# One of two row scalings of a retention output moved from the retention stage into the attention stage of a hybrid encoder block

## The chip, the cores and the metric

The kernel runs on one core of a Trainium2 chip. A core has five engines, each with an instruction queue of its own that it works off in order: PE (TensorE, matrix products), DVE (VectorE), ACT (ScalarE), POOL (GpSimd) and SP (SyncE, which here issues all DMAs). They wait for one another by semaphores. The metric is the device time of one execution in microseconds; the median of three runs is given.

## The reference

One encoder block over 1024 frames plus 16 meta tokens, model width 1024, float32. The input is normalised and projected to a retention group (4 heads, key width 64, value width 128) and a forgetting-attention group (8 heads of width 64); their outputs stand side by side in a mixer output of width 1024 that is projected back. A gated feed-forward network with a short convolution and a last normalisation follow.

```python
def hybrid_mixer(h, w_in, forget_b, ret_norm_g, w_out, valid):
    proj = jnp.einsum('bld,de->ble', h, w_in)
    rq, rk, rv, rg, fq, fk, fv, ff = jnp.split(proj, SPLIT_POINTS, axis=-1)
    o_r = retention(rq..., rk..., rv..., valid)              # (B, L, 4, 128)
    o_r = o_r * lax.rsqrt(jnp.mean(o_r * o_r, axis=-1, keepdims=True) + EPS)
    o_r = o_r.reshape(B, L, RET_V) * ret_norm_g * jax.nn.silu(rg)
    log_f = jax.nn.log_sigmoid(ff + forget_b)
    o_f = forgetting_attention(fq..., fk..., fv..., log_f, valid)
    mixed = jnp.concatenate([o_r, o_f], axis=-1)
    return jnp.einsum('ble,ed->bld', mixed, w_out)
```

The change concerns the factor `rsqrt(mean(o_r * o_r))` of head 1. The kernel keeps `o_r` transposed, 128 value features on the partitions and time along the free axis, so this factor is one row of 1026 numbers (the 1024 frames and the two positions ahead of them that the convolution reaches back to) that multiplies all 128 partitions.

## The kernel before, in words

All matrix products are made in float32 precision from two parts: a rounded high part and the difference to it, the low part, in three products (high by high, high by low, low by high). ACT makes the high parts, DVE or POOL the low parts.

The program has these stages, in order of time.

1. **Projections and retention of heads 0 and 1** (`retention(0, ...)`), to about 95 us.
2. **Gates of heads 0 and 1** (`gate(0, ...)`, `gate(1, ...)`) with the end of the first retention (`fin()`): it squares each head's output, sums the squares over the partitions on POOL (`head_sum`, L241, PARTITION_ALL_REDUCE, in halves of 513), and turns the sums into the row `ro` of reciprocal roots by a trip through DRAM (`head_rstd`, L247 to L250). `gate` writes the gated head, not yet scaled, to the DRAM tensor `mix`.
3. **Row scalings** (`scale_rows`, L525 to L530) of heads 0 and 1: load `mix` (tile `sraw`), load the row `ro` repeated on all partitions (tile `src`), multiply on POOL (L529), store to the DRAM tensor `mixg`. Both tiles come from `stage`, a pool of two buffers. Head 1's tiles therefore take the buffers of head 0's.
4. **Retention of heads 2 and 3** (`retention(1, ...)`), from about 105 to 195 us. It runs over four blocks of time (the first one with an extra tile of 16 meta tokens). Per block it projects with `rv_hi`/`rv_lo` into `psj` (L183 to L185), turns and rotates queries and keys, multiplies keys with queries into `psq` (L355, L356), weighs the scores by the decay on DVE (`sf`, two buffers, L361), splits them into `sh` (ACT) and `sl` (POOL, L118), and multiplies these with the values into `psv` (L376 and L377 with `sh`, L378 with `sl`).
5. **Forgetting attention** (from about 195 us), with the projections of its heads spread between its steps (`dense`, L667 and after). It begins with the column sums of heads 2 and 3 on POOL, whose result tiles come from the two buffers of the tag `o`; later the heads' outputs `o` use the same two buffers. `prep_k`, `prep_q` and `max_step` prepare head 0; `load_m` reads all rows of `mixg` near the stage's end.
6. **Rest of the output projection, feed-forward network and last normalisation**, from about 560 us to the end.

Stages 1 to 4 are put in order by a scheduler, which simulates the engines with costs of its own and takes what is ready; so a change of one engine's work changes how the others' queues are interleaved. In stages 5 and 6 the queues of PE, DVE, ACT and POOL keep the order of the program text, while SP's DMAs are still placed by the scheduler.

Of the kernel before, what the change touches and what calls it, by code (L numbers as in the profile page):

```python
# [10 lines left out]
F32 = mybir.dt.float32  # L11
# [6 lines left out]
P = 128  # L18
# [4 lines left out]
NQ = NT - Q0  # L23
# [58 lines left out]
def tile_hymba_block(ctx, tc, xt, xn, wrv0, wrv1, wft, wout, wup, wdn, small, cst, rope, dtab, out):  # L82
# [3 lines left out]
    def f(t):  # L86
        return t.bitcast(F32)

    def mk(es, name, bufs=1, **kw):
        return es.enter_context(tc.tile_pool(name=name, bufs=bufs, reuse_waits="tile", **kw))  # L90
# [10 lines left out]
    def bank(pl):  # L101
        n = names[id(pl)]
        return pl.tile([P, 512], F32, tag=n, name=n)
# [47 lines left out]
    def stage(nm, dt=F32):  # L151
        return sp_.tile([P, NT], dt, tag="st", name=nm)
# [87 lines left out]
    def head_sum(h, rs_, sq, c_):  # L240
        pool.partition_all_reduce(rs_, sq, P, bass_isa.ReduceOp.add)  # L241
        sp.dma_start(ro_d[h][:, c_], rs_[0:1, :])
# [271 lines left out]
    def gate(h, gt, o, late=False):  # L514
        for ps, (a, n) in proj_t(load_ft(f"rg{h}", (dve, pool)[GL[h]], lx[-1] if h == 0 else None), CX_Q, Q0):
            dve.tensor_tensor(gt[:, a:a + n], ps, rb[:, Q0 + a:Q0 + a + n], op=ALU.mult)
        act.activation(gt, gt, AF.Silu)
        if late:
            sp.dma_start(o, ro_d[h].to_broadcast([P, NQ]))
            dve.tensor_tensor(gt, gt, o, op=ALU.mult)  # L520
            sp.dma_start(o, mix_d[h])
        dve.scalar_tensor_tensor(gt, gt, sm[:, S_RG + h:S_RG + h + 1], o, op0=ALU.mult, op1=ALU.mult)
        sp.dma_start(mixg_d[h] if late else mix_d[h], gt)

    def scale_rows(k):  # L525
        raw, rc = stage("sraw")[:, :NQ], stage("src")[:, :NQ]
        sp.dma_start(raw, mix_d[k])
        sp.dma_start(rc, ro_d[k].to_broadcast([P, NQ]))
        pool.tensor_tensor(raw, raw, rc, op=ALU.mult)  # L529
        sp.dma_start(mixg_d[k], raw)  # L530
# [5 lines left out]
    def w_dma(u):  # L536
        if u < len(units_w):
            nm = units_w[u]
            src = wout[int(nm[2])] if nm[:2] == "wo" else wft[:, FX[nm]:FX[nm] + KT * P]
            raws[u] = []  # L540
            for hf in range(2):
                n = (NA - 4) * P if nm[:2] == "wo" and int(nm[2]) < EARLY and hf else 512
                raw = wf.tile([P, 512], F32, tag="raw", name="f_raw", bufs=RB)
                sp.dma_start(raw[:, :n], src[:, hf * 512:hf * 512 + n])
                raws[u].append((raw, n // P))
# [2 lines left out]
    fin()  # L548
    wt1 = [load_rv(1, wr, bb, k) for k in range(KT)]
    gate(1, stage("gate")[:, :NQ], ots[1])  # L550
    for k in range(2):
        scale_rows(k)
    w_dma(0)
    retention(1, wt1, None)[0]()
    ra.close()
# [11 lines left out]
    fp = mk(fa, "fp", 1, side="right")  # L567
# [7 lines left out]
    for s in range(2):  # L575
        o = 64 - 64 * s
# [17 lines left out]
    def w_split(u):  # L594
        if u < len(units_w):
            wts[u] = []
            for raw, n in raws.pop(u):
                h = wg.tile([P, 4, P], F32R, tag="fh", name="f_hi")
                l = wg.tile([P, 4, P], F32R, tag="fl", name="f_lo")
                split(h[:, :n], l[:, :n], raw.rearrange("p (a b) -> p a b", b=P)[:, :n], dve)  # L600
                wts[u].append((h, l))
# [96 lines left out]
    def prep_k(h):  # L698
        p, s = divmod(h, 2)
        h_, o_ = HS[s], HS[1 - s]  # L700
        prep_c(h)
        act.copy(kB[s][h_], kst[p][h_])
        dve.tensor_tensor(k1[s][o_], kst[p][h_], f(kB[s])[h_], op=ALU.subtract)
        dup[0] = sp.dma_start(f(k1[s])[h_], f(kB[s])[h_])
# [8 lines left out]
    def prep_q(h):  # L713
        p, s = divmod(h, 2)
        h_, o_ = HS[s], HS[1 - s]
        c = slice(Q0, NT)
        act.copy(q1[s][h_, c], qst[p][h_, c])
        sp.dma_start(f(qm[s])[h_, c], f(q1[s])[h_, c])
        dve.tensor_tensor(qB[s][h_, c], qst[p][h_, c], f(q1[s])[h_, c], op=ALU.subtract)
        dup[0] = sp.dma_start(f(q1[s])[o_, c], f(q1[s])[h_, c])  # L720

    def max_step(h, j):
        s = h % 2
        t0, R = KTILES[j]
        q_ = Q0 if j == 0 else 0
        w = min(NT, P * j + P)
        for ci, a in enumerate(range(0, w, 512)):
            n = min(512, w - a)
            last = a + n == w
            ps = bank(pS)  # L730
            pe.matmul(ps[:R - q_, :n], lhsT=qm[s][:, t0 + q_:t0 + R], rhs=kB[s][:, a:a + n], start=True, stop=not last)  # L731
            if last:
                pe.matmul(ps[:R - q_, n - R:n], lhsT=msk[:, q_:R], rhs=idr[:, :R], start=False, stop=True)
            dve.tensor_reduce(mxs[s][:R - q_, j, ci:ci + 1], ps[:R - q_, :n], axis=mybir.AxisListType.X, op=ALU.max)  # L734

    def max_end(h):
        s = h % 2
        mf = fp.tile([P, 9], F32, tag="mf", name="mf", bufs=2)
        dve.tensor_reduce(mf, mxs[s], axis=mybir.AxisListType.X, op=ALU.max)
        m2 = fp.tile([P, 2, 9], F32R, tag="m2", name="m2", bufs=2)  # L740
        dve.tensor_scalar(m2[:, 0, :], mf, -1.0, None, op0=ALU.mult)
        dve.scalar_tensor_tensor(m2[:, 1, :], mf, -1.0, f(m2)[:, 0, :], op0=ALU.mult, op1=ALU.subtract)
        return m2

    def max_rows(h, m2):
        s = h % 2
        T = bank(pT)
        pe.transpose(T[:18, :P], f(m2).rearrange("p a b -> p (a b)"), idf)
        mr = fp.tile([18, P], F32, tag="mr", name="mr", bufs=1)
        act.copy(mr, T[:18, :P])  # L750
        sp.dma_start(md[s].rearrange("i (j p) -> (i j) p", p=P), mr)
        o = 64 - 64 * s + 3
        sp.dma_start(f(qB[s])[o:o + 2, Q0:P], md[s][:, 0:P - Q0])
        dup[0] = sp.dma_start(f(qB[s])[o:o + 2, P:NT], md[s][:, P:NT])
# [176 lines left out]
    def run(upto):  # L931
        while done[0] < upto:
            c = next(dn, 0)
            if c == 0:
                done[0] = 1 << 60
            done[0] += c
# [12 lines left out]
    with tc.manual_schedule(engines=ENG):  # L949
        for s_ in range(2):  # L950
            rs_ = fp.tile([P, NQ], F32, tag="o", name="rss", bufs=2)
            head_sum(2 + s_, rs_, sqs[s_], slice(0, NQ))
        w_split(0)
        run(U + 161)
        prep_q(0)
        run(2 * U + 1)
        prep_k(0)
        for j in range(9):
            run(2 * U + V * (j + 5) // 15)
            max_step(0, j)  # L960
        run(2 * U + V * 14 // 15)
        m2 = max_end(0)
        prep_k(1)
        prep_q(1)
        run(2 * U + V + 1 + U // 8)
        max_rows(0, m2)
        run(GOAL[0])
        for h in range(2, 4):
            head_rstd(h)
        for t in range(len(units) + LAG):  # L970
            h, at = divmod(t, NU)
            if h < 7:
                want = GOAL[h] + (GOAL[h + 1] - GOAL[h]) * (at + 1) // NU
            else:
                want = GOAL[7] + (END - GOAL[7]) * (t - 7 * NU + 1) // (NU + LAG)
            run((done[0] + want) // 2)
            if h == 6 and at == 4:
                fqs.close()
                wA[0] = mk(fqs, "wA", side="right")
            if h == 6 and at == 4:  # L980
                m7 += [mt[7][:, 0, :], mt[7][:, 1, :]]
            if h == 6 and at == 12:
                load_m(6, mt[6])
            if h == 7 and at == 4:
                split_m(6)
            if t < len(units):
                part_s(t)
            if 0 <= t - 1 < len(units):
                part_d(t - 1)
            if 0 < h and at == 6:  # L990
                norm1(h - 1)
            if 0 < h and at == 10:
                norm2(h - 1)
            if t < len(units):
                if h < 7:
                    if at == 0 and h > 0:
                        prep_q(h + 1)
                    if at == 1 and h > 0:
                        prep_k(h + 1)
                    for j in range(9):  # L1000
                        if SPLIT[j] == at:
                            max_step(h + 1, j)
                    if at == SPLIT[8]:
                        m2 = max_end(h + 1)
                    if at == SPLIT[8] + 1:
                        max_rows(h + 1, m2)
            run(want)
            if t - LAG >= 0:
                part_v(t - LAG)
        run(1 << 50)  # L1010
# [826 lines left out]
```

## Time and profile before

| | |
|---|---|
| timed runs | 1337.38, 1339.93, 1330.31 us; median 1337.38 |
| profiled execution | 1337.85 us, of it the span from first to last instruction 1334.9 us |
| PE busy | 1272.2 us (95% of the span) |
| DVE, ACT, POOL busy | 925.9, 588.0, 378.0 us |
| mean granted PE clock | 0.972 |
| the two row scalings on POOL | 2.39 us at 125.77 and 2.34 us at 137.59 |

In a row of a timeline stand the start and the length in us, the engine, the line of the kernel, the operation, output `<-` inputs, the shapes, and in brackets how long the engine had been idle before and what released it. "issue" as a releaser means that the profile shows none. A row of waits has who waited, for whom, the total in us, how often, and the longest. The granted clock is the share of full speed at which PE was allowed to run.

### The profile page before, as it was taken

The page shows a single profiled execution, that of the slowest core. Times are in us where ns is not written, and L with a number is a line of the kernel's source. Part 1 is how long each engine was busy: PE and PEld are TensorE (multiplying, and loading weights), DVE is VectorE, ACT ScalarE, POOL GpSimd, SP SyncE. Part 2 cuts the span into 40 slices and gives each one's busy share as a digit, 9 for nine tenths or more (in the row PEclk, how much of TensorE's full clock was granted, in tenths as well). Part 3 has the DMA queues.
Part 4 walks back from the last instruction along what each step waited for, and adds up shares of the span by engine and source line. Part 5 has one row for each costly group of instructions (what it writes and reads, how often), then busy time and mean ns, then how long its engine had stood idle before and what let it go on. Part 6 is the DMA issues. An engine that isn't in the chain of part 4 may idle for free.

```text
span 1334.9 us, 24161 instructions
## 1 busy us (share of the span) xinstructions
PE 1272.2 (95%) x9243; PEld 1202.9 (90%) x9243; DVE 925.9 (69%) x1573; ACT 588.0 (44%) x1162; POOL 378.0 (28%) x308
## 2 busy tenths in 40 slices
PE   9999799999999989988799999999999998999995
PEld 8999799999999989977699999999999997888884
DVE  5774456555665666647878878879889885955566
ACT  7763251445355554532443433433433435444553
POOL 0163235000000000033336545546546540500123
PEclk9999699999999999998899999999999998999998
DMA  8533112122224435274145345446566579766533
GB/s 289 166 110 101 46 53 74 42 57 73 81 65 105 142 92 155 83 229 133 41 135 171 123 141 175 128 134 217 174 203 204 178 238 332 257 205 194 195 107 126
DMA packets 110946, 192.75 MB, mean 144 GB/s; under 512 B 15143, under 2 KB 50295, under 8 KB 110832
## 3 DMA queue, kind: packets, MB, share of 16 engines
q1 hardware_dynamic: 110832, 191.23, 45.5%
q8 instruction: 72, 1.18, 0.4%
q14 instruction: 42, 0.34, 0.1%
HBM read 132.59 MB, written 52.21 MB: 138 GB/s over the span
## 4 chain that ended last, share of the span: by engine, by line
PE 43%; DVE 4%; issue 1%; DMA 1%; ACT 1%; POOL 0%; SPq 0%; DVEq 0%; ACTq 0%; POOLq 0%
PE psb L1287 12%; PE psc L1287 9%; PE psa L1287 8%; PE psc L1438 4%; PE psa L1438 4%; PE psx L1438 3%; PE psb L1438 3%; DVE d_u L1263 1%; DMA uB<-u 1%; DMA d_raw<-uB 1%; DVE Hp L1147 0%; DVE fo L1708 0%; DVE B1T L1153 0%; DVE sd L1169 0%; DVE unit L1263 0%
## 5 line engine op out<-in xcount | busy, mean ns | idle before, releaser
L1263 DVE TENSOR_TENSOR d_u<-d_raw,d_u 128x512 fp32r<-128x512 f32 x154 | 118.0, 819 | 61.6 <-ACT d_u L1262 61.6
L667 PE MATMUL psD<-xh,f_hi 128*128 128x256 f32 (+2 forms) x448 | 129.5, 289 | 1.8 <-DVE fk L675 1.3
L1262 ACT CAST d_u<-d_raw 128x512 fp32r<-128x512 f32 x154 | 87.4, 619 | 99.2 <-PE psc L1438 45.7
L667 PE MATMUL psD<-xl,f_hi 128*128 128x256 f32 (+2 forms) x448 | 130.3, 291 | 0.0
L667 PE MATMUL psD<-xh,f_lo 128*128 128x256 f32 (+2 forms) x448 | 129.2, 288 | 0.0
L1258 POOL TENSOR_TENSOR S<-u_raw 128x512 f32<-128x512 f32 x44 | 64.3, 1461 | 196.3 <-DVE unit L1263 194.7
L1287 PE MATMUL psb<-B1T,unit 128*128 128x256 f32 x780 | 102.5, 280 | 2.7 <-DVE at L1303 2.7
L1287 PE MATMUL psb<-B0T,unit 128*128 128x256 f32 x780 | 103.8, 282 | 0.5 <-DVE bt L1309 0.3
L798 ACT ACTIVATE pf<-psS 128x272 f32<-128x272 f32 (+4 forms) x112 | 49.6, 450 | 114.1 <-PE psS L788 69.7
L1287 PEld LDWEIGHTS psb<-B1T,unit 128*128 128x128 f32 x780 | 96.8, 190 | 3.0 <-ACT B1T L1150 3.0
L1287 PEld LDWEIGHTS psb<-B0T,unit 128*128 128x128 f32 x780 | 97.5, 190 | 0.9 <-issue 0.5
L1262 ACT CAST unit<-S 128x512 fp32r<-128x512 f32 x87 | 54.2, 623 | 77.6 <-PE psb L1287 75.1
L667 PEld LDWEIGHTS psD<-xh,f_hi 128*128 128x128 f32 x448 | 85.9, 192 | 2.7 <-DVE fk L675 1.2
L1444 POOL MEMSET on<- 128x128 f32 x1 | 0.2, 204 | 309.9 <-PE psS L792 309.9
L667 PEld LDWEIGHTS psD<-xl,f_hi 128*128 128x128 f32 x448 | 85.6, 191 | 0.4
L667 PEld LDWEIGHTS psD<-xh,f_lo 128*128 128x128 f32 x448 | 85.6, 191 | 0.1
L1263 DVE TENSOR_TENSOR unit<-S,unit 128x512 fp32r<-128x512 f32 x87 | 81.0, 931 | 6.4 <-ACT unit L1262 6.4
L734 DVE TENSOR_REDUCE mx<-psS 128x1 f32<-128x512 f32 (+6 forms) x120 | 59.0, 538 | 30.1 <-PE psS L731 20.8
L183 PE MATMUL psj<-rv_hi,xh 128*128 128x256 f32 (+1 forms) x264 | 77.0, 296 | 1.6 <-DVE z L287 1.2
L185 PE MATMUL psj<-rv_hi,xl 128*128 128x256 f32 (+1 forms) x264 | 76.7, 293 | 0.0
L184 PE MATMUL psj<-rv_lo,xh 128*128 128x256 f32 (+1 forms) x264 | 76.7, 292 | 0.0
L1438 PE MATMUL psa<-d_u 128*128 128x512 f32 (+1 forms) x282 | 69.2, 383 | 5.1 <-DVE d_u L1263 3.9
(343 smaller groups left out, 3575.7 us busy)
## 6 DMA issues: line engine op xcount, KB each, us to landing
u_raw<-wup SPq DMA_DIRECT2D x44, 512.0 KB
sd<-wdn SPq DMA_DIRECT2D x88, 128.0 KB
uB<-u SPq DMA_DIRECT2D x44, 256.0 KB
wS<-sd SPq DMA_DIRECT2D x88, 128.0 KB
d_raw<-wS SPq DMA_DIRECT2D x44, 256.0 KB
d_raw<-uT SPq DMA_DIRECT2D x44, 256.0 KB
d_raw<-wdn SPq DMA_DIRECT2D x33, 256.0 KB
d_raw<-uB SPq DMA_DIRECT2D x33, 256.0 KB
```

Of the source, the lines that this page charges most:

```text
L183: pe.matmul(ps[:, :w], lhsT=x_h, rhs=w_h[:, c0:c0 + w], start=(k == 0), stop=False)
L184: pe.matmul(ps[:, :w], lhsT=x_h, rhs=w_l[:, c0:c0 + w], start=False, stop=False)
L185: pe.matmul(ps[:, :w], lhsT=x_l, rhs=w_h[:, c0:c0 + w], start=False, stop=(k == KT - 1))
L667: pe.matmul(ps[:, :n], lhsT=w_, rhs=X(e, k, t0 + a, n), start=(k == 0 and i == 0), stop=(k == KT - 1 and i == 2))
L734: dve.tensor_reduce(mxs[s][:R - q_, j, ci:ci + 1], ps[:R - q_, :n], axis=mybir.AxisListType.X, op=ALU.max)
L798: act.activation(pf[:r, a:b], ps[:r, a:b], AF.Exp)
L1258: pool.tensor_tensor(t, s_[x], s_[y], op=o)
L1262: act.copy(t[:, 0], src)
L1263: eng.tensor_tensor(t[:, 1], src, f(t[:, 0]), op=ALU.subtract)
L1287: pe.matmul(ps[:, :n], lhsT=w[:, wi, k * P:(k + 1) * P], rhs=o[:, hl, k, :], start=(new and k == 0 and j == 0), stop=(k == 3 and j == 2), ...
L1438: pe.matmul(ps[:, c:c + n], lhsT=a_[:, wi, j * P:(j + 1) * P], rhs=b_[:, hl, c:c + n], start=(new and m == 0), stop=(kt == KH - 1 and m == ...
L1444: pool.memset(on, 1.0)
```

## The change

`scale_rows` gets the place of its tiles as an argument. Head 0 is scaled where it was. Head 1 is scaled in the text of the attention stage, behind `max_rows(0, m2)`, with tiles of the tag `o` instead of `stage`. The same loads, product and store are made. Lines behind L552 move up by one as far as the inserted line.

```diff
-    def scale_rows(k):
-        raw, rc = stage("sraw")[:, :NQ], stage("src")[:, :NQ]
+    def scale_rows(k, buf):
+        raw, rc = buf("sraw")[:, :NQ], buf("src")[:, :NQ]
         sp.dma_start(raw, mix_d[k])
         sp.dma_start(rc, ro_d[k].to_broadcast([P, NQ]))
         pool.tensor_tensor(raw, raw, rc, op=ALU.mult)
@@
-    for k in range(2):
-        scale_rows(k)
+    scale_rows(0, stage)
     w_dma(0)
     retention(1, wt1, None)[0]()
@@
         max_rows(0, m2)
+        scale_rows(1, lambda n: fp.tile([P, NQ], F32, tag="o", name=n, bufs=2))
         run(GOAL[0])
```

On POOL, at the start of the second retention, the queue before had both products (`x2`) ahead of the first `sl`:

```order
L241 ISA rss<-rsq 128x513 x4
L529 ISA
L529 TENSOR_TENSOR sraw<-sraw,src 128x1026 x2
L118 TENSOR_TENSOR sl<-sf,sh 16x258
L118 TENSOR_TENSOR sl<-sf,sh 128x256
L118 TENSOR_TENSOR sl<-sf,sh 128x128
```

Now one of them stands there, and the other behind the column sums of heads 2 and 3:

```order
L529 ISA
L529 TENSOR_TENSOR sraw<-sraw,src 128x1026
L118 TENSOR_TENSOR sl<-sf,sh 16x258
...
L241 ISA
L241 ISA rss<-rsq 128x1026 x2
L529 ISA
L529 TENSOR_TENSOR sraw<-sraw,src 128x1026
L1444 MEMSET on 128x128
```

The second product has moved past all the `sl` of the second retention and the fills of the attention's tiles; the row "ISA" ahead of it is the switch of POOL's configuration. The next row in the queue, the fill of `on`, belongs to stage 6.

On PE, at the first block of the second retention, the queue before had 21 projection matmuls (`psj`) between a score matmul (L356) and the first matmul on a low half (L378); the rows where they begin and end:

```order
L355 MATMUL psq<-qb,kb 128x256
L356 MATMUL psq<-qz_121,kb 128x256
L185 MATMUL psj<-rv_hi,xl_99 128x256
L183 MATMUL psj<-rv_hi,xh_98 128x256
...
L184 MATMUL psj<-rv_lo,xh_98 128x256
L378 MATMUL psv<-sl,vn 128x258
L376 MATMUL psv<-sh,vn 128x256
```

Now:

```order
L356 MATMUL psq<-qz_121,kb 128x256
L378 MATMUL psv<-sl,vn 128x258
L185 MATMUL psj<-rv_hi,xl_99 128x256
L376 MATMUL psv<-sh,vn 128x256
L377 MATMUL psv<-sh,vn 128x256
L355 MATMUL psq<-qb,kb 128x128
L356 MATMUL psq<-qz_121,kb 128x128
L183 MATMUL psj<-rv_hi,xh_98 128x256
L184 MATMUL psj<-rv_lo,xh_98 128x256
L185 MATMUL psj<-rv_hi,xl_99 128x256
L378 MATMUL psv<-sl,vn 128x256
```

The matmuls on the low halves have moved ahead of the projections. The interleaving of PE, DVE and ACT differs from here up to the last block of the second retention and is the same again behind that, line numbers aside.

On SP, at the start of the attention, the part of the queue with the loads of weights (`f_raw`) and the trips of the column sums (`ro`, `rst`) before:

```order
L242 DMA ro_532<-rss 1x1026
L544 DMA f_raw<-wft 128x512
L247 DMA rst<-ro_532 114x9
L544 DMA f_raw<-wft 128x512
L242 DMA ro_533<-rss 1x1026
L704 DMA k_2923<-kB_2925 64x1040
L247 DMA rst<-ro_533 114x9
L544 DMA f_raw<-wft 128x512 x2
L704 DMA k_2924<-kB_2926 64x1040
```

Now:

```order
L242 DMA ro_532<-rss 1x1026
L544 DMA f_raw<-wft 128x512
L527 DMA sraw<-mix_70 128x1026
L544 DMA f_raw<-wft 128x512
L247 DMA rst<-ro_532 114x9
L242 DMA ro_533<-rss 1x1026
L703 DMA k_2917<-kB_2919 64x1040
L528 DMA src<-ro_531 128x1026
L247 DMA rst<-ro_533 114x9
L544 DMA f_raw<-wft 128x512
L530 DMA mixg_1455<-sraw 128x1026
L544 DMA f_raw<-wft 128x512
```

The two loads and the store of the scaling stand among them, the store between the two halves of one weight.

## The prediction

> **What bounds the kernel now.** I read the page first, then the waits around the place of the change, then the timelines of the queues there, then the granted clock by stretches.
>
> ```profile
> span 1334.9 us, 24161 instructions
> PE 1272.2 (95%) x9243; PEld 1202.9 (90%) x9243; DVE 925.9 (69%) x1573; ACT 588.0 (44%) x1162; POOL 378.0 (28%) x308
> ```
>
> TensorE (PE) is busy 95% of the span, so a change counts by what it does to PE's idle time and to PE's clock. The waits between 126 and 141 us, where the two row scalings run, name one large hole (columns: who waited for whom, total us, times, longest):
>
> ```profile
> POOL sraw L529 <- issue: 16.7, 2, 9.4
> PE psv L378 <- POOL sl L118: 7.8, 1, 7.8
> ```
>
> PE stands 7.8 us for `sl`, the low half of a score tile that POOL makes. POOL's and SP's timelines (start, length, what) say why:
>
> ```profile
> 115.17 3.27 POOL L241 PARTITION_ALL_REDUCE rss<-rsq  x1 [4.76 <-DMA ro<-rss]
> L529 POOLq MODIFY_POOL_CONFIG  x2: 89/89/89, 118.4 to 118.4; - x2
> 125.77 2.39 POOL L529 TENSOR_TENSOR sraw<-sraw,src 128x1026 f32<-128x1026 f32 x1 [7.32 <-issue]
> 137.59 2.34 POOL L529 TENSOR_TENSOR sraw<-sraw,src 128x1026 f32<-128x1026 f32 x1 [9.43 <-issue]
> 139.89 2.01 POOL L118 TENSOR_TENSOR sl<-sf,sh 16x258 fp32r<-16x258 f32 x3
> ...
> 128.19 0.32 SPq L530 DMA_DIRECT2D mixg<-sraw  x1
> 128.56 0.42 SPq L527 DMA_DIRECT2D sraw<-mix  x1
> 133.79 0.32 SPq L528 DMA_DIRECT2D src<-ro  x1
> ```
>
> The second product stands in POOL's queue ahead of the first three `sl`. It reuses the two staging buffers, so its loads go out only when the first row has been scaled and written (128.56 and 133.79). POOL waits 9.43 us for them with the `sl` queued behind. PE runs out of other work and then runs slowly. Its timeline and the windows (length, busy and count of PE, PEld, DVE, ACT, POOL, then PE's granted clock, DMA) read:
>
> ```profile
> 140.66 0.58 PE L378 MATMUL psv<-sl,vn 16*128 16x258 f32 x1 [7.78 <-POOL sl L118]
> ...
> 132.88:140.66 7.78, 0.00 (x1) 0.00 (x0) 0.02 (x1) 0.00 (x0) 3.07 (x3) 0.70 0.21 68
> 140.66:156.30 15.64, 15.64 (x64) 14.17 (x65) 7.68 (x24) 5.18 (x17) 3.17 (x5) 0.50 0.19 59
> 156.52:188.00 31.48, 31.48 (x272) 31.48 (x272) 19.69 (x59) 13.98 (x43) 5.09 (x8) 1.00 0.03 8
> 194.65:200.56 5.91, 5.91 (x27) 5.91 (x28) 0.00 (x0) 3.50 (x5) 5.66 (x7) 0.50 0.56 217
> ```
>
> After the hole the clock is at 0.50 for 15.64 us, in which PE does 64 matmuls; at clock 1.00 it does 272 in 31.48 us, 0.116 us each.
>
> **The change part by part.** The profiled execution took 1337.85 us, its span plus 2.95; the median of the three timed runs is 1337.38, half a microsecond lower, so the sum is made on 1337.85. 1% is 13.4 us, about what a measurement of this kernel can tell from no change.
>
> *Stall removed.* POOL now takes the `sl` straight behind the first product, which ends at 128.16. PE's queue moves with it: the first matmul on `sl` stands right behind the score matmul that ran at 130.10, 21 matmuls earlier than before. Is `sl` there in time? The rows that feed it:
>
> ```profile
> 127.39 0.41 ACT L117 CAST sh<-sf 128x256 fp32r<-128x256 f32 x1 [0.67 <-DVE sf L361]
> 130.10 0.28 PE L356 MATMUL psq<-qz,kb 128*128 128x256 f32 x1
> ```
>
> Three `sl` took 2.01 us, 0.67 each. The first is then ready at 128.16 + 0.67 = 128.83, needed at about 130.2; the second (its `sh` ended at 127.80) at 129.5, needed nine matmuls on. The third waits for the `sf` buffer that the first frees, and comes near 130.1, with four matmuls more in front of it. So the 7.78 us go, and next late is nothing in this block: the margin is 1.4 us on the first. In the blocks after it, PE ran 272 matmuls in 31.48 us without a gap, and the distances in the queue there are alike. **Gain 7.8.**
>
> *Slow clock removed.* Without the hole the 64 matmuls cost 64 x 0.116 = 7.4 us instead of 15.64. **Gain 8.2.** Its lower bound is the shorter slow stretch after a smaller disturbance, 194.65 to 200.56: half of 5.91, about 3.
>
> [...]
>
> *Product added in the attention.* Behind the two column sums of heads 2 and 3 POOL is idle, so the 2.37 us of the product are free on POOL itself. It starts when POOL has switched from the column sum (7.32 us in the row at 125.77) and `src` has landed. In the old times the rows are:
>
> ```profile
> 210.26 12.95 POOL L241 PARTITION_ALL_REDUCE rss<-rsq  x2 [6.22 <-issue]
> 224.98 0.26 SPq L247 DMA_DIRECT2D rst<-ro  x1
> 230.13 1.28 DVE L118 TENSOR_TENSOR f_lo<-f_raw,f_hi 128x512 fp32r<-128x512 f32 x2
> 231.33 2.40 DVE L734 TENSOR_REDUCE mx<-psS 128x1 f32<-128x512 f32 x5
> 234.44 1.16 DVE L734 TENSOR_REDUCE mx<-psS 128x1 f32<-128x512 f32 x2 [0.23 <-PE psS L731]
> 238.62 0.42 DVE L613 TENSOR_TENSOR vaL<-psT,vaH 128x256 fp32r<-128x256 f32 x1 [0.20 <-ACT vaH L612]
> 239.70 1.24 DVE L703 TENSOR_TENSOR k<-fk,kB 64x1040 fp32r<-64x1040 f32 x1 [0.16 <-ACT kB L702]
> 242.80 0.52 PE L607 MATMUL psT<-idf,vst 128*128 128x128 f32 x3 [1.65 <-DVE vst L675]
> ```
>
> The sums end at 223.2 (two in one row), plus 7.3 gives 230.5. `src` goes out beside the `rst` at 224.98, which waits for the same landing, and needs the 3.8 us that lay between 133.79 and 137.59: 228.8, so the switch comes last. At 230.5 VectorE (DVE) is in the two `f_lo`, which read two SBUF tiles, and it has almost no slack up to 242, where PE already waits 1.65 us for it. Does a POOL product slow such an instruction? Two rows of one instruction beside `sl`, one of a column sum (it ran beside 210.26) and its undisturbed sister:
>
> ```profile
> 143.28 0.84 DVE L296 TENSOR_TENSOR rt<-rt,rt 128x256 f32<-128x256 f32 x1
> 146.22 0.43 DVE L296 TENSOR_TENSOR rt<-rt,rt 128x256 f32<-128x256 f32 x1
> 211.10 4.80 DVE L719 TENSOR_TENSOR qB<-fq,q 64x1026 fp32r<-64x1026 f32 x1 [1.12 <-ACT q L717]
> 240.97 1.23 DVE L719 TENSOR_TENSOR qB<-fq,q 64x1026 fp32r<-64x1026 f32 x1
> ```
>
> It does: 0.84 against 0.43, 4.80 against 1.23. Bounds: 0 if the product falls among the `mx` reductions, which read one PSUM tile; 2.37, its whole length, if an `f_lo` waits it out. Less the DVE gaps of 0.23 + 0.20 + 0.16 = 0.59 up to 242 that is 1.8; I take it, since 230.5 lies inside the `f_lo` row. **Cost 1.8.**
>
> [...]
>
> *DMAs moved.* The load of `sraw`, the load of `src` and the store of `mixg` now stand among the loads of attention weights on SP. What is queued behind the store is the second half of an `f_raw` and `k<-kB`:
>
> ```profile
> 230.84 0.96 SPq L544 DMA_DIRECT2D f_raw<-wft  x2
> 239.69 0.47 SPq L704 DMA_DIRECT2D k<-kB  x1
> 244.90 1.12 ACT L117 CAST f_hi<-f_raw 128x512 fp32r<-128x512 f32 x2
> ```
>
> The store goes out at 230.5 + 2.4 = 232.9, so the half moves from 231.3 to 233.3; ACT first reads the pair at 244.90. **Cost 0**, with 11 us of cover. The scaled row is read only when the output projection's inputs load, two heads later. The new tile's buffers come from the `o` pair, and head 0 writes `o` at 256.95 at the earliest by ACT's timeline, long after the store:
>
> ```profile
> 256.95 0.36 ACT L840 COPY o<-psO 128x242 f32<-128x242 f32 x1 [0.32 <-PE psO L825]
> ```
>
> Sum: 7.8 + 8.2 - 1.8 = 14.2; 1337.85 - 14.2 = 1323.7, on the median's scale 1323.2. Everything behind 242 moves forward together, since PE's waits there are on DVE and ACT work of the same stage.
>
> **The rivals.**
>
> *PE goes cold at 242 (chance 0.26).* The hole of 1.65 us grows by 1.8 to 3.5. Shorter holes have done it and not done it:
>
> ```profile
> 483.98 0.49 PE L895 MATMUL psD<-m,f_hi 128*128 128x342 f32 x1 [1.14 <-DVE m L118]
> 485.00:487.00 2.00, 2.00 (x9) 2.00 (x9) 0.73 (x3) 0.00 (x0) 0.00 (x0) 0.50 0.00 0
> ...
> 1318.83 0.71 PE L1687 MATMUL pr<-dg,on 128*128 128x128 f32 x4 [2.40 <-DVE dg L1686]
> 1319.00:1322.00 3.00, 2.70 (x22) 2.49 (x22) 0.80 (x3) 0.79 (x2) 0.00 (x0) 1.00 0.00 0
> ```
>
> 1.14 us did, 2.40 us did not. The price is half of a slow stretch of 5.91 us: 3.0. Gain 11.2, time 1326.
>
> *The slow clock is worth 3 instead of 8.2 (0.12).* [...] Against it stands that the profiled run agrees with the median; for it, that one timed run is at 1330.31.
>
> *The stall stays in another place (0.10).* The first product still stands ahead of the `sl`. If the new order asks for some tile too early, the hole opens again behind another wait, and the time is 1337. The margin of 1.4 us above speaks against it.
>
> *Slower: the weights wait behind the store (0.06).* SP works in order. If the store of `mixg` waits on POOL beyond 244.90, each microsecond is one of PE's, and a long hole costs the 8.2 of the slow clock again. It ends slower than before from 16.0 - 8.2 = 7.8 us beyond that, so from a store at about 253; at 260 it would be 1345. The longest way from the issue of a `src` to its product is below 10.2 us (issued 115.59, product 125.77, rows of SP and POOL), which gives a store at 237.6.
>
> ```profile
> 115.59 0.34 SPq L528 DMA_DIRECT2D src<-ro  x1
> ```
>
> That the change does not do what it says is out: the order shows one product moved and nothing else added.
>
> **How the numbers follow.** The forecast has 0.46, the rivals 0.26, 0.12, 0.10 and 0.06. The forecast's own range is 1316 to 1327: without the DVE block 16.0 is gained (1321.4), the slow stretch at 194.65 may also fall away (3 more), and the three timed runs lie 7.1 below to 2.6 above their median. The range 1315 to 1331 adds the first two rivals and leaves out the last two, with 0.16, and edges. Faster by over 1% means below 1324.0: about 0.39 of the forecast's 0.46, a third of the first rival and a little of the second, 0.50. Slower 0.05, the rest 0.45.
>
> **What would show it.** Right: no PE wait on `sl` L378 over 1 us between 125 and 145; clock 1.00 from 125 to the end of that retention; retention's last block about 16 us earlier; one L529 product some 7 us behind the last column sum, a DVE `f_lo` of over 2 us beside it, and a PE wait on `vst` of about 3.5 us. Wrong: a slow clock behind that wait (first rival), another wait of several us before 160 (third), an ACT wait on `f_raw` (the last).

## The result

| | before | after |
|---|---|---|
| timed runs | median 1337.38 us (1330.08 to 1348.67, 11 runs) | median 1324.15 us (1319.96 to 1329.79, 11 runs) |
| profiled execution (span) | 1337.85 us (1334.9) | 1325.43 us (1323.6) |
| POOL product of head 1 | at 137.59 | at 218.22 |

The changed kernel takes 0.9901 of the time before, with an interval of 0.9874 to 0.9929: 13.2 us less. 1323.2 was predicted. So the time came out nearly right. Its parts did not all, and the experiments below show which.

The top of the profile of the changed kernel, then the row of TensorE's (PE) waits on `sl` between 118 and 200 us, then its first matmul on `sl` in the second retention and a window of 20 us that begins 2.7 us ahead of it (length, busy and count of PE, granted clock, DMA share, GB/s). Here and below, rows of a timeline between those shown are left out:

```profile
span 1323.6 us, 24163 instructions
PE 1267.7 (96%) x9243; PEld 1198.8 (91%) x9243; DVE 920.3 (70%) x1573; ACT 588.7 (44%) x1162; POOL 376.7 (28%) x308
```

```profile
PE psv L378 <- POOL sl L118: 0.9, 3, 0.3
```

```profile
132.99 0.38 PE L378 MATMUL psv<-sl,vn 16*128 16x258 f32 x1
```

```profile
130.29:150.29 20.00, 20.00 (x161) 1.00 0.15 47
```

The hole of 7.78 us is gone (three waits of 0.3 us each are left, in the retention's last block, where the kernel before has three too), and the clock stays at 1.00. In POOL's timeline the three `sl` now stand directly behind the first product, and the second product behind the column sums:

```profile
128.87 2.40 POOL L529 TENSOR_TENSOR sraw<-sraw,src 128x1026 f32<-128x1026 f32 x1 [7.39 <-issue]
131.25 1.93 POOL L118 TENSOR_TENSOR sl<-sf,sh 16x258 fp32r<-16x258 f32 x3
198.61 12.37 POOL L241 PARTITION_ALL_REDUCE rss<-rsq  x2 [6.95 <-ACT f_hi L117]
218.22 2.40 POOL L529 TENSOR_TENSOR sraw<-sraw,src 128x1026 f32<-128x1026 f32 x1 [7.24 <-issue]
```

Beside that product VectorE's (DVE) timeline reads:

```profile
214.75 1.28 DVE L118 TENSOR_TENSOR f_lo<-f_raw,f_hi 128x512 fp32r<-128x512 f32 x2
215.95 2.41 DVE L733 TENSOR_REDUCE mx<-psS 128x1 f32<-128x512 f32 x5
218.41 0.42 DVE L612 TENSOR_TENSOR vaL<-psT,vaH 128x256 fp32r<-128x256 f32 x1
219.07 1.16 DVE L733 TENSOR_REDUCE mx<-psS 128x1 f32<-128x512 f32 x2 [0.23 <-PE psS L730]
220.14 0.41 DVE L674 TENSOR_TENSOR vst<-psD,rb 128x256 f32<-128x256 f32 x1
224.01 0.17 DVE L741 SCALAR_TENSOR_TENSOR m<-mf,m 128x9 fp32r<-128x9 f32 x1
```

The product runs from 218.22 to 220.62. The two `f_lo` were over at 216.03 and took 1.28 us, as before. What lies beside the product are the `mx` reductions out of PSUM and two steps that read one input from PSUM and one from SBUF (`vaL`, `vst`), all as long as before to 0.01 us: the reductions 2.41 for 2.40 and 1.16 for 1.16, the two steps 0.42 and 0.41 in both. Four places in PE's timeline let both traces be laid side by side: the wait on `vst` in the attention, one on `m` in its middle, one on `Hp` in the output projection, one on `dg` near the end.

```profile
227.43 0.52 PE L606 MATMUL psT<-idf,vst 128*128 128x128 f32 x3 [1.64 <-DVE vst L674]
468.51 0.42 PE L894 MATMUL psD<-m,f_hi 128*128 128x342 f32 x1 [1.13 <-DVE m L118]
611.41 0.95 PE L1065 MATMUL psa<-m,wo 128*128 128x512 f32 x3 [3.74 <-DVE Hp L1077]
1307.60 0.71 PE L1687 MATMUL pr<-dg,on 128*128 128x128 f32 x4 [2.39 <-DVE dg L1686]
```

The same rows stood at 242.80, 483.98 and 1318.83 before, and the one on `Hp` here:

```profile
625.56 0.79 PE L1065 MATMUL psa<-m,wo 128*128 128x512 f32 x1 [3.73 <-DVE Hp L1077]
```

So the changed kernel is ahead by 15.4 us at the `vst` wait, 15.5 at 468, 14.2 at the `Hp` wait and 11.2 at the end. It also began its retention late: the first product is at 128.87 against 125.77, 3.1 us behind. Some 18.5 us were gained between there and the attention, and about 4 given back after 580. The wait on `vst` stayed at 1.64 us.

### The profile page after: what moved, and what is told of

Same layout as the page of the kernel before. It is cut to its first block, busy times and chain, and to the rows that moved or that the text cites. A ratio compares the mean times of both kernels' runs of the same rounds, so it can differ in the third digit from the quotient of the medians.

```text
span 1323.6 us, 24163 instructions
## 1 busy us (share of the span) xinstructions
PE 1267.7 (96%) x9243; PEld 1198.8 (91%) x9243; DVE 920.3 (70%) x1573; ACT 588.7 (44%) x1162; POOL 376.7 (28%) x308
## 4 chain that ended last, share of the span: by engine, by line
PE 81%; DVE 8%; DMA 4%; ACT 3%; issue 2%; POOL 1%; SPq 1%; DVEq 0%; ACTq 0%; POOLq 0%
PE psb L1287 14%; PE psD L666 11%; PE psc L1287 9%; PE psa L1287 9%; PE psO L824 4%; PE psc L1438 4%; PE psa L1438 4%; PE psD L894 3%; PE psx L1438 3%; PE psb L1438 3%; PE psS L787 3%; PE psS L730 2%; PE psj L183 2%; PE psj L185 2%; PE psj L184 2%
```

## The experiments

The theory to be tested: PE waits, and then runs slowly, only because the second product stands on POOL between the column sums and the first `sl`. Rivals: the two heads' shared staging tiles are the cause; the new place has a price; what differs between the traces at the start and after 580 us belongs to the change. All ratios are to the kernel before, run beside them on the same chip (medians 1334.78, 1336.70 and 1336.9 us in three such comparisons). Line numbers shift by one or two between kernels.

**Own tiles for head 1, at the old place.**

```diff
-    for k in range(2):
-        scale_rows(k)
+    scale_rows(0, stage)
+    scale_rows(1, lambda n: gp.tile([P, NQ], F32, tag="g", name=n))
```

> Both scalings stay in the retention as before, but head 1's tiles are no longer those of head 0: they come from the pair of retention output tiles. Theory A (what cost the time is POOL's queue: the second product stands ahead of the first sl and cannot start before its row of factors has gone through SP's queue, whose step of that row stands behind the store of head 0): PE still waits 4 to 8 us for sl and the slow clock follows; 1330 to 1337 us. Theory B (the shared pair of staging tiles alone made the second product late): the second product runs right behind the first, sl is 2.4 us late, PE waits at most 1 to 2 us, no slow clock; about 1324 us, as the changed kernel.

Measured: 1335.05 us, ratio 1.0003 (0.9978 to 1.0029). Its timelines of SP, of POOL and of PE:

```profile
128.94 0.32 SPq L530 DMA_DIRECT2D mixg<-sraw  x1
129.36 0.28 SPq L250 DMA_DIRECT2D ro<-rst  x1
132.91 0.32 SPq L528 DMA_DIRECT2D src<-ro  x1
```

```profile
136.59 2.34 POOL L529 TENSOR_TENSOR sraw<-sraw,src 128x1026 f32<-128x1026 f32 x1 [7.68 <-DMA src<-ro]
138.89 1.91 POOL L118 TENSOR_TENSOR sl<-sf,sh 16x258 fp32r<-16x258 f32 x3
```

```profile
139.67 0.58 PE L378 MATMUL psv<-sl,vn 16*128 16x258 f32 x1 [6.44 <-POOL sl L118]
```

Tiles of its own free head 1's loads of the staging buffers, but not of SP's queue. The last write of head 1's factors (`ro<-rst`, 129.36) stands behind the store of head 0's product, which waits for POOL until 128.94, and the load of `src` behind both. So the product still starts at 136.59, and the hole is 6.44 us. The shared tiles are one lock of two, and opening one gains nothing.

**The new place with the old tiles.**

```diff
-    for k in range(2):
-        scale_rows(k)
+    scale_rows(0, stage)
@@
         max_rows(0, m2)
+        scale_rows(1, stage)
         run(GOAL[0])
```

> The place is changed alone: head 1's scaling stands in the attention as in the changed kernel but keeps the two staging tiles, which the attention's v and gate tiles also use. Theory A (the place brings the whole gain): same as the changed kernel within 3 us, 1321 to 1327. Theory B (the new tiles are needed, since the staging tiles hold up the projections of the attention): a wait of PE on vst of over 2 us between 205 and 230 us and 1328 or more.

Measured: 1326.7 us, ratio 0.9945 (0.9927 to 0.9964). There is no wait of PE on `sl` above 0.3 us, so the place, and not the choice of other tiles, removes the hole. Here the product ran later, at 232.94, and the wait on `vst` was 1.64 us as well, at 227.41 for 227.43 in the changed kernel. The ratio lies 0.4% above the changed kernel's 0.9901, and the intervals just touch; whether the other tiles are worth a part of that stays open.

**Products put back in front of `sl`, one, two and three.** Head 0's row scaling gets further products of the same size behind its store, which nobody reads.

```diff
-    def scale_rows(k, buf):
+    def scale_rows(k, buf, extra=0):
@@
         sp.dma_start(mixg_d[k], raw)
+        for _ in range(extra):
+            pool.tensor_tensor(rc, raw, rc, op=ALU.mult)
@@
-    scale_rows(0, stage)
+    scale_rows(0, stage, 1)     # 2 and 3 in the other two
```

> The changed kernel with one more product of the same size on GpSimd between head 0's row scaling and the first sl (the row factors are multiplied once more, and nobody reads that result). The theory that TensorE waits for sl only because GpSimd gets to it late: sl comes 2.4 us later than in the changed kernel, in which it had something over 1 us to spare, so the wait of TensorE is 0 to 2 us, too short for a slow clock, and the time is 1 to 2 us above the changed kernel's (ratio to the kernel before about 0.991 to 0.994, against 0.999 with three products more). The rival, that any further GpSimd work in this place brings the whole loss back: a wait of 4 us or more and slow clock behind it, ratio 0.997 to 1.001.

> The changed kernel with two more products of GpSimd between head 0's row scaling and the first sl, between the doses of one (TensorE's wait on sl 0.41 us, no slow clock, no loss) and three (5.97 us, slow clock to 10 us, the whole gain lost). The wait should be 2.8 to 3.5 us, since each product is 2.4 us. If the slow clock follows with the length of the wait, a stretch of 3.4 to 6.8 us behind it: 1325 to 1330 us, ratio 0.993 to 0.996. If a wait of some 3 us leaves the clock alone: the wait alone is lost, ratio 0.991 to 0.993. If any wait of that size costs the full slow stretch: ratio 0.996 to 0.999.

> The changed kernel, with three more products of the same shape (2.4 us each, their results unused) on POOL between head 0's scaling and the first sl. Theory A (what PE lost is set by how late POOL comes to sl, and the slow clock follows the hole): sl is 7.2 us later, less 1.4 us of margin and less what the scheduler puts ahead of it; PE waits 3 to 6 us and the clock falls to 0.50 for 6 to 16 us, 6 to 13 us slower than the changed kernel. Theory B (it was the wait on DMAs, not POOL's lateness): no more than 2 us slower.

PE's row at the first `sl`, and then the window of 20 us that begins there, with one product:

```profile
130.29 0.38 PE L378 MATMUL psv<-sl,vn 16*128 16x258 f32 x1 [0.41 <-POOL sl L118]
```

```profile
130.29:150.29 20.00, 20.00 (x163) 1.00 0.08 24
```

With two:

```profile
137.42 0.58 PE L378 MATMUL psv<-sl,vn 16*128 16x258 f32 x1 [3.99 <-POOL sl L118]
```

```profile
137.42:157.42 20.00, 20.00 (x141) 0.86 0.07 21
```

With three:

```profile
139.22 0.58 PE L378 MATMUL psv<-sl,vn 16*128 16x258 f32 x1 [5.96 <-POOL sl L118]
```

```profile
139.22:159.22 20.00, 20.00 (x139) 0.84 0.07 21
```

The time that the clock costs in a window is its length times what the clock lacks to 1.00, so 0, 20 x 0.14 = 2.8 and 20 x 0.16 = 3.2 us. Wait and clock together are 0.4, 6.8 and 9.2 us.

| extra products | wait on `sl` | lost to the clock | time | ratio |
|---|---|---|---|---|
| none (changed kernel, second time) | three of 0.3 | 0 | 1322.69 us | 0.9899 (0.9867 to 0.9932) |
| one | 0.41 | 0 | 1321.93 us | 0.9899 (0.9867 to 0.9931) |
| two | 3.99 | 2.8 | 1326.88 us | 0.9919 (0.9888 to 0.9951) |
| three | 5.96 | 3.2 | 1334.76 us | 0.9993 (0.9962 to 1.0023) |

One product more costs nothing that the time shows: it opens 0.41 us, where the prediction's margin of 1.4 us would have left 1.0. That a wait of up to 2 us is too short for a slow clock was my estimate, and no such bound was shown: behind 1.14 us at 483.98 the kernel before has a clock of 0.50, behind 2.40 at 1318.83 one of 1.00. Three take the whole gain back, with SP's loads and stores there in the same order. So it is enough that POOL comes late to `sl`. PE's queue is not the same in all of them: with one and two products the first matmul on `sl` follows the score matmul directly, as in the changed kernel, and with three the scheduler puts four projections between them. Ratio and trace do not fit closely either: two products cost 6.8 us by wait and clock, but only 4 us of median; three cost 9.2 us so, but 12 us of median, with runs from 1326.69 to 1341.31 us.

**Head 1 not scaled at all.**

```diff
-        sp.dma_start(mixg_d[h] if late else mix_d[h], gt)
+        sp.dma_start(mixg_d[h] if late or h == 1 else mix_d[h], gt)
@@
-        scale_rows(1, lambda n: fp.tile([P, NQ], F32, tag="o", name=n, bufs=2))
```

> Head 1's row scaling is left out altogether (the unscaled head is stored where the scaled one belongs), all else as in the changed kernel. Theory A (the moved product costs nothing in the attention): same time as the changed kernel, 1322 to 1326, and the wait of PE on vst near 226 us stays at 1.6 us. Theory B (the moved product, its loads and its store cost what was forecast, 1.8 us, or more through the clock): 1.8 to 5 us less than the changed kernel.

Measured: 1322.25 us, ratio 0.9925 (0.9894 to 0.9955), and the same wait of 1.7 us on `vst`. Without the product, its loads and its store the kernel is no faster than with them in the new place. These times alone could not tell a cost of 1.8 us (0.1%, with an interval of 0.6%); that PE's wait is the same with and without them says that the product holds PE up by nothing there.

**Four products at the new place.** The moved product is followed by three more that nobody reads, behind its store.

```diff
-        scale_rows(1, lambda n: fp.tile([P, NQ], F32, tag="o", name=n, bufs=2))
+        scale_rows(1, lambda n: fp.tile([P, NQ], F32, tag="o", name=n, bufs=2), 3)
```

> The changed kernel with three more products of GpSimd directly behind the moved one in the attention part; they come behind the store, so that nothing on SyncE's queue waits for them, and nobody reads their results. They fill GpSimd to some 7 us past the first product (about 219 to 226 us), beside VectorE's reductions, its L702 and L718 and the vst copy for which TensorE waits 1.64 us. The prediction's term of 1.8 us for one product would give up to 5 us for three more: the vst wait at 3.5 us or more, ratio 0.993 to 0.996. The reading of the changed kernel's trace, that a product of GpSimd costs VectorE's reductions out of PSUM nothing: the vst wait at 1.6 to 2.4 us and a ratio of 0.988 to 0.992, the same as the changed kernel.

Measured: 1329.77 us, ratio 0.9950 (0.9928 to 0.9971). Its timelines of POOL, of DVE and of PE, and the window behind the first wait:

```profile
218.04 2.39 POOL L529 TENSOR_TENSOR sraw<-sraw,src 128x1026 f32<-128x1026 f32 x1 [9.23 <-DMA rst<-ro]
220.50 7.33 POOL L532 TENSOR_TENSOR src<-sraw,src 128x1026 f32<-128x1026 f32 x3
```

```profile
222.06 2.58 DVE L735 TENSOR_REDUCE mx<-psS 128x1 f32<-128x512 f32 x5
225.59 2.26 DVE L743 SCALAR_TENSOR_TENSOR m<-mf,m 128x9 fp32r<-128x9 f32 x1
```

```profile
228.00 0.27 PE L749 MATMUL psT<-idf,m 128*18 128x128 f32 x1 [1.10 <-DVE m L743]
230.98 0.87 PE L608 MATMUL psT<-idf,vst 128*128 128x128 f32 x3 [2.34 <-DVE vst L676]
```

```profile
228.00:236.00 8.00, 5.66 (x35) 0.79 0.40 79
```

The reductions took 2.58 us for five, as in the changed kernel. The tiny step L743 (L741 there, 0.17 us) took 2.26 and ended at 227.85, when the last product ended (220.50 + 7.33 = 227.83). Its two inputs lie in SBUF. In this trace it was the first step of that kind to start while a product ran; the two small steps ahead of it (L740 and L742, each with one input in SBUF) took 0.17 us each beside the same products. PE then waits 1.10 + 2.34 = 3.44 instead of 1.64 us, with 8 x 0.21 = 1.7 us of slow clock on top, 3.5 us in all. So a price like the one I forecast is there in this trace, and it fell on one of the instructions beside the products and not on the others. The median is 5.6 to 7.1 us above the changed kernel's two, up to twice what this place explains. The rest I leave open: this trace also loses about 3 us between 185 and 210, ahead of the products, and has a long slow stretch after 616, of which more below.

Two other traces show the same kind of meeting. With both heads at the new place (next) the second product ran from 228.55 to 230.93, and two `f_lo` beside it took 2.68 us instead of 1.28. That is the meeting which the prediction had counted on:

```profile
229.40 2.68 DVE L118 TENSOR_TENSOR f_lo<-f_raw,f_hi 128x512 fp32r<-128x512 f32 x2
```

With the old tiles at the new place a step `P` of VectorE (at 234.39) took 1.66 us beside the product (232.94 to 235.64), and 0.55 us in the changed kernel.

**Both heads at the new place.**

```diff
-    scale_rows(0, stage)
@@
+        scale_rows(0, lambda n: fp.tile([P, NQ], F32, tag="o", name=n, bufs=2))
         scale_rows(1, lambda n: fp.tile([P, NQ], F32, tag="o", name=n, bufs=2))
```

> Both heads' row scalings stand at the place in the attention part (head 0's goes there too, in the same kind of tiles, ahead of head 1's), so GpSimd has no product and no wait for their loads between the column sums and sl. If the rest of the row scaling still held TensorE up at the start of the retention, this gains again on the changed kernel; by the trace of the changed kernel it holds nobody up (no wait on sl there), so the theory expects no gain at the retention, and at the new place a second product of about 2.4 us and two more loads and one more store on SyncE's queue: 0.988 to 0.993 of the kernel before, the same as the changed kernel within what can be measured. The rival, that two products of GpSimd beside VectorE cost there what I had expected of one, or that the stores delay the weights behind them: 2 to 5 us slower than the changed kernel, ratio 0.992 to 0.996.

Measured: 1332.72 us, ratio 0.9984 (0.9956 to 1.0011), worse than either expectation. Its timelines of SP and of PE, and the window of 8 us behind PE's wait:

```profile
223.49 0.32 SPq L528 DMA_DIRECT2D src<-ro  x1
230.95 0.32 SPq L530 DMA_DIRECT2D mixg<-sraw  x1
232.64 1.13 SPq L749 DMA_DIRECT2D md<-mr  x1
236.36 0.25 SPq L751 DMA_DIRECT2D qB<-md  x1
```

```profile
238.22 0.54 PE L786 MATMUL psS<-qB,kB 128*128 128x242 f32 x1 [8.13 <-DMA qB<-md]
```

```profile
238.22:246.22 8.00, 8.00 (x53) 0.76 0.27 66
```

The second store waits for POOL's second product until 230.95, and behind it in SP's queue stand `md` and `qB`, for which PE then waits 8.13 us; the slow clock adds 8 x 0.24 = 1.9. Those 10 us are the loss (1332.72 us against 1322.69 of the changed kernel in the same comparison). At the retention the trace shows the waits on `sl` of the changed kernel (three of 0.3 us), so moving head 0 gains nothing there. This is the prediction's slower rival, with `qB` for the weights.

**The same without the second store.** Head 1's unscaled rows go to `mixg` and are loaded from there; the scaled ones are not stored.

```diff
-        sp.dma_start(mixg_d[h] if late else mix_d[h], gt)
+        sp.dma_start(mixg_d[h] if late or h == 1 else mix_d[h], gt)
@@
-        sp.dma_start(raw, mix_d[k])
+        sp.dma_start(raw, (mix_d, mixg_d)[k][k])
@@
-        sp.dma_start(mixg_d[k], raw)
+        if k == 0:
+            sp.dma_start(mixg_d[k], raw)
```

> As the kernel with both row scalings in the attention part, but head 1's scaled rows are not stored (its unscaled rows are stored in their place by the step that makes them, and loaded from there), so head 1's gate result goes unscaled into the output projection. Loads and both products stay. If the loss of that kernel comes from SyncE's queue, where the store waits for GpSimd's second product and md and qB wait behind the store (TensorE waits 8.1 us for qB), it goes with the store: md leaves SyncE 6 to 8 us earlier, TensorE's wait for qB is 0 to 2.5 us, ratio 0.989 to 0.994. If it comes from the second product's work beside VectorE, or from the loads, the wait stays at 5 us or more, ratio 0.996 to 1.000.

Measured: 1328.09 us, ratio 0.9944 (0.9925 to 0.9962). The waits of SP between 200 and 240 us, then PE's row:

```profile
SPq L528 <- DMA mixg<-sraw: 4.0, 1, 4.0
```

```profile
235.34 0.35 PE L787 MATMUL psS<-qB,kB 128*128 128x242 f32 x1 [3.26 <-DMA qB<-md]
```

PE's wait lies between the two expectations: the store was 4.9 of the 8.13 us. In what is left SP stands 4.0 us before the second load of `src`, because that tile comes free only when the first store has landed. That is again a wait on SP's queue ahead of `md`, by the same two tiles; it is the likely cause of the 3.26 us, but was not taken away by itself.

**The kernels before and after, profiled again.**

> The kernel before, profiled a second time. Two readings of the slow clock behind the wait on the sl tiles. Fixed: the hole of 7.8 us costs the same slow clock again, 15.6 us at 0.50 behind its end (about 8 us lost), and the later slow stretches stand where they stood (about 6.8 us each at 600, 624 and 658, with none of 13 us or more). Drawn anew in each execution: the stretch behind the hole is another multiple of about 3.4 us (6.8 or 10.2 more likely than 15.6, since two other kernels with the same hole showed 9.4 and 6.8), and the stretch near 625 may be 13 to 17 us in this kernel too. The wait itself should be 5.9 to 7.8 us by either.

> The kernel before, profiled a third time. If the length of the slow clock behind the wait on sl belongs to this kernel, it is 20.5 us again as in the two profiles so far; if it is drawn anew, another multiple of 3.4 us (10.2 or 13.6, as in the kernels whose wait was about 6 us). The stretch behind the wait on Hp (6.8 us in the first profile, 13.6 us in the second) may be anything from 3.4 to 17 us.

> The changed kernel again, beside the runs of this call. By the account that the place of the row scaling is the whole cause: no wait of TensorE on sl between 120 and 195 us, and a ratio to the kernel before of 0.988 to 0.993. If the stretch of slow clock near 619 to 637 us (17 us in the first profile of this kernel) belongs to the change, it is there again with 13 us or more; if it is drawn anew in each execution, it is a different multiple of 3.4 us, and the time of the profiled run follows it (about 1.7 us for each 3.4 us of slow stretch).

The changed kernel again: 1322.69 us, ratio 0.9899 (0.9867 to 0.9932), no wait on `sl` over 0.3 us. The kernel before, second profile, PE's row at the first `sl` and the 20 us behind it:

```profile
142.00 0.58 PE L378 MATMUL psv<-sl,vn 16*128 16x258 f32 x1 [7.12 <-POOL sl L118]
```

```profile
142.00:162.00 20.00, 20.00 (x99) 0.59 0.15 47
```

Third profile:

```profile
144.93 0.58 PE L378 MATMUL psv<-sl,vn 16*128 16x258 f32 x1 [7.96 <-POOL sl L118]
```

```profile
144.93:164.93 20.00, 20.00 (x142) 0.88 0.15 47
```

And the same window of the first profile:

```profile
140.66:160.66 20.00, 20.00 (x101) 0.60 0.15 47
```

So the clock cost 8.0, 8.2 and 2.4 us in one and the same kernel: the kernel alone does not set it. The 25 us behind the wait on `Hp`, first of the kernel before in its three profiles in order, then of the changed one in its two (one row from each trace):

```profile
625.56:650.56 25.00, 23.37 (x149) 0.82 0.46 148
...
625.90:650.90 25.00, 24.93 (x135) 0.66 0.45 148
...
623.59:648.59 25.00, 24.93 (x133) 0.65 0.44 148
```

```profile
611.41:636.41 25.00, 25.00 (x125) 0.60 0.44 148
...
609.72:634.72 25.00, 23.34 (x156) 0.86 0.44 148
```

Both kernels have both kinds, short (0.82, 0.86) and long (0.60 to 0.66). What the first pair of traces gives back there is the draw of two executions, not the change. So is part of the 18.5 us: near 195 us the kernel before is slow for 6.8 us in its first two profiles and for 3.4 in its third, the changed kernel (from 183 and 180 us on) for 3.4 in both (summed over windows of 1 us); at a clock of 0.50 the 3.4 us more cost 1.7. The same holds for the start: the second product's predecessor, at 125.77 in the first profile before and 128.87 in the first one after, is at 126.40 in the second one after.

## Why the prediction was right, and where it was not

**Stall removed (7.8): right.** The hole was 7.78, 7.12 and 7.96 us in three profiles of the kernel before and is absent from both of the changed kernel. The products put back show that POOL's lateness is enough to bring it back, and the margin of 1.4 us held about: the first of the three `sl` ended near 131.9 (131.25 and a third of 1.93) and PE took it at 132.99, 1.1 us later; in the second profile it is 1.5.

**Slow clock removed (8.2): the cause was right, the size was that of one execution.** All of it goes with the hole: the clock is 1.00 over the 20 us in both profiles of the changed kernel. But 8.0, 8.2 and 2.4 us were lost in three profiles, 6.2 in the mean, so the first profile showed the dear case. Its lower bound, 3 us from the short stretch at 194.65, was nearly the third profile. I priced that as a rival of its own (7.8 + 3.0 - 1.8 = 9.0, time 1328.5), as if one length or the other held; in fact both happen to the same kernel.

**Product added (1.8): failed, PE's wait shows a cost of 0** (1.64 us for 1.65). The step that failed is the meeting. I let the product start at 230.5 in the old times, inside the two `f_lo`. They now stood 15.4 us earlier (214.75 for 230.13), but the column sums only 12.2 (their end 210.98 for 223.21), so the product met the reductions and two steps with one SBUF input instead. The time between the sums and the product was right, 7.24 us for the 7.3 I had taken. The bound of 0 with its condition was in the prediction, the value taken was the other one. That a meeting of the other kind does cost, the four products (2.26 us for 0.17) and the `f_lo` of 2.68 us for 1.28 show.

**DMAs moved (0): right, but for a cover that I did not name.** I looked at `f_raw` and 11 us. The near victim is `qB`, behind `md`: the kernel with both scalings there loses 8.13 us on it.

**The sum.** Wait and clock behind it make 15.8, 15.3 and 10.4 us in the three profiles of before, 13.8 in the mean; the medians moved by 13.2 and, in the later comparison, by 14.0. With a cost of 0 at the new place these two terms account for the gain, as closely as three profiles between 10.4 and 15.8 can say. My 14.2 was 16.0 less 1.8: one term too dear by about 2, the other by 1.8, with opposite signs. That the total was within a microsecond is partly luck.

**The rivals.** PE's clock did not fall behind the `vst` wait: the wait stayed at 1.64 us, and the clock was 1.00 from 228 to 236. The stall did not open elsewhere. A slow clock that costs about 3 us was there in one of three profiles of before (2.4). The store did not block the weights, but the experiment with two stores shows the block itself.

**What was to be seen:** no wait on `sl` over 1 us, clock 1.00 up to the retention's last matmul on `sl`, a product some 7 us behind the column sums: all there. The retention's last block about 16 us earlier: that last matmul starts at 182.67 for 195.35, so 12.7 us earlier, or 15.8 with the late start of 3.1 us added. An `f_lo` of over 2 us beside the product and a `vst` wait of 3.5: not there.

## To carry to other kernels

An instruction on a side engine is free only as long as what stands behind it in that engine's queue, and in the queue that feeds it, is not the next thing TensorE needs; move it behind the last such piece of work, and then look at what its store holds up at the new place (one row scaling there held TensorE up by nothing, two cost 10 us). A wait of TensorE of several us can cost more than its length, but the slow clock behind it must be taken from several profiles: one and the same hole cost 2.4 to 8.2 us. Whether two engines cost each other time depended here on which instructions met (beside a product of POOL five `mx` reductions kept their 2.58 us, and two `f_lo` took 2.68 instead of 1.28), so give such a cost by its condition and not by the one meeting that the old times show.

## What the runs showed of the hardware

The clock did not come back soon in spite of continuous matmuls: behind the hole PE was busy for 20.00 of 20 us in all three profiles of before, at a mean clock of 0.59 to 0.88. In the changed kernel it was busy for all of the 25 us behind the `Hp` wait, at 0.60; but there the clock had come back to 1.00 (616.50 to 619.00) and fell again while PE ran 48 matmuls of one column each (`psx`, from 617.28), so that stretch is not all owed to the wait. Summed over windows of 1 us, the slow stretches (from inside the hole on) were near multiples of 3.4 us long: 6.8 behind the hole of 3.99 us, 10.2 behind that of 5.96, 13.6 behind 6.44, and 20.5, 20.5 and 10.2 in the three profiles of before. A single stretch of 3.4 us at 0.50 stands in the changed kernel from 182.9 us on. What sets the length these runs do not show: for a hole of nearly 8 us it was 20.5 in one profile and 10.2 in another.
